# Output projection of a transformer block as seven half-size products, with weight sums made during attention

## The chip, the cores and the metric

One core of a Trainium2 chip runs the whole kernel. The metric is device time in microseconds (us). A core has five engines with instruction queues of their own, each worked through in order: TensorE (PE in the profile; its weight loads are PEld), VectorE (DVE), ScalarE (ACT), GpSimd (POOL) and SyncE (SP), which here issues all DMAs. PSUM, where matmuls accumulate, has eight banks of 128 x 512 fp32 each.

## The reference

An encoder block for 1024 tokens and a model width of 1024, all in fp32. Sixteen meta tokens are put ahead of the sequence and dropped at the end.

```python
def mixer_block(h, w_in, lq1, lk1, lq2, lk2, subln_g, sink, w_ba, w_bb, w_o, lambda_init):
    proj = h @ w_in
    ...
    y_a = differential_attention(...)      # 4 heads: softmax(s1) - lam * softmax(s2), times v
    y_b = windowed_gqa(...)                # 8 heads in a window
    merged = jax.nn.sigmoid(ga) * (y_a @ w_ba) + jax.nn.sigmoid(gb) * (y_b @ w_bb)
    return merged @ w_o

def swiglu(h, w_gate, w_up, w_down):
    return (jax.nn.silu(h @ w_gate) * (h @ w_up)) @ w_down

    # in reference():
        h = h + mixer_block(rms_norm(h, norm_mix[layer]), ...)
        h = h + swiglu(rms_norm(h, norm_ffn[layer]), ...)
    return rms_norm(h, norm_final)[:, N_META:]
```

The change concerns `merged @ w_o`, a product of 1024 x 1024 by 1024 x 1024, and the stages beside it.

## The kernel before

**Numbers.** Every fp32 operand of a large product is kept as a high and a low half in `fp32r`. `split(hi, lo, src, engine)` makes them: ACT copies the high half (L117), the named engine subtracts it from the source to get the low half (L118). Each product is three matmuls: high by high, high by low, low by high.

**Seven products for eight.** The gates (`pg`, L737), the FFN (`product_f`, `pg`, L1293) and the down-projection (`pd`, L1387) are done as 2 x 2 block products with seven half-size multiplications in place of eight (Winograd's form), for which sums of blocks are made of both operands. Before the change the output projection is not: it is a plain product, 8 row tiles x 2 column halves x 8 chunks x 3 = 384 matmuls of 128x512 (`po`, L1070).

**Stages**, in the order of TensorE: projections and branch B's attention (0 to about 322 us); branch A's attention, four heads of eight tiles, interleaved with the gates' matmuls (322 to 622); the branch B product, 16 groups of 12 matmuls (`ppa`, L780); the branch A product, 16 groups, with the merge; the output projection (709 to 801); for each of eight row tiles the second norm and its turn, the transposition into FFN operands (`norm_f`, `turn_f`, `ptn_f`); the FFN in steps of 14 x 11 products with the operands `b` and their sums `t`; the down-projection to the end at 1444.

**A tile of branch A.** TensorE makes scores (`aps`), VectorE takes them with their row maxima, ACT makes the exponentials `as` (L804), POOL scales one of the two maps by lambda (L807), VectorE joins the maps (L810), TensorE transposes the result (`apt`, L822), ACT and VectorE copy it as high and low halves `at` (L825, L826), and TensorE multiplies by the values (`apy`, L835). At the start of a head 30 gate matmuls fill the time in which its first scores pass through the other engines.

**The merge.** For each group `gated` loads a tile of gate logits (`gt`), ACT takes the sigmoid, and VectorE multiplies with the PSUM bank (L1041). POOL adds branch B's part (L1042), and `split` makes the halves of the merged tile `mT`.

**Order.** TensorE's order is the order of the program text from branch A on (`manual_schedule`). ACT, POOL, SP and, before the change, VectorE are ordered by the framework's scheduler, which models the times; the chip then keeps that order. SP's queue is one queue: a DMA that waits holds those behind it. Weight tiles pass through a ring of five raw tiles and eight operand tiles.

The functions that the change touches follow, with the line numbers of the profile.

## Time and profile before

| | |
|---|---|
| Time, median of 3 runs | 1448.48 us (1448.33 to 1451.66) |
| Profiled execution | 1446.1 us, span 1444.3 us |
| Granted TensorE clock | 0.997 |
| Busy: PE, DVE, ACT, POOL | 1422.8, 899.2, 679.6, 641.3 us |
| `po`, output projection | 384 matmuls, 88.0 us |
| `ppa`, branch B and branch A products | 384 matmuls, 622.4 to 709.5 us |

The times are of whole runs; the span is that of the one execution which was profiled. Busy time counts instructions of an engine without its waits. A row of grouped instructions names the line, engine, operation and tiles, then how many, the busy time, the mean of one in ns, and the idle time before them with what ended it. A row of the timeline begins with its start and its length in us.

### The profile page before, as it was taken

Reading aid. Unit: us, or ns where it says so; the run is one execution under the profiler, and the core shown is the slowest. Engines: PE = TensorE matmul, PEld = TensorE weight load, DVE = VectorE, ACT = ScalarE, POOL = GpSimd, SP = SyncE. Lnnn points to the kernel's source line nnn. Section 1 sums busy time; section 2 is a strip of 40 time slices with the busy share of each in tenths; the row PEclk is TensorE's granted clock in tenths of the full one; section 3 lists DMA queues with packets and bytes.
Section 4 is the critical chain, followed back from the end, with each engine's and each line's share of the span. In section 5 each row is a group of like instructions: output and inputs, shape, how many; then the busy total and the mean of one; then the engine's idle time right before and its main releaser. Section 6 shows DMA issues by size and latency. Waiting matters only on the chain.

```text
span 1444.3 us, 21160 instructions
## 1 busy us (share of the span) xinstructions
PE 1422.8 (99%) x7279; PEld 1221.2 (85%) x7279; DVE 899.2 (62%) x1624; ACT 679.6 (47%) x1290; POOL 641.3 (44%) x605
## 2 busy tenths in 40 slices
PE   8999999999999999999999999999999999999997
PEld 6988989988898999888888878888888888888886
DVE  7478536637697989624614966554555553787567
ACT  6366535545665656544413643333333333444454
POOL 5599127743333333334522665544544452000444
PEclk9999999999999999999999999999999999999999
DMA  8467658986557473576612534333332332964443
GB/s 244 90 209 237 193 162 265 288 281 213 190 169 257 147 227 125 190 256 209 216 34 88 152 104 161 109 102 110 102 102 96 110 102 102 331 208 140 124 129 139
DMA packets 188891, 242.41 MB, mean 168 GB/s; under 512 B 18208, under 2 KB 115936, under 8 KB 188784
## 3 DMA queue, kind: packets, MB, share of 16 engines
q1 hardware_dynamic: 188784, 241.07, 52.6%
q8 instruction: 57, 0.93, 0.3%
q14 instruction: 50, 0.41, 0.1%
HBM read 157.45 MB, written 77.00 MB: 162 GB/s over the span
## 4 chain that ended last, share of the span: by engine, by line
PE 81%; POOL 6%; DVE 5%; issue 4%; DMA 2%; ACT 1%; POOLq 0%; SPq 0%; DVEq 0%; ACTq 0%
PE pg L1293 28%; PE pd L1387 9%; PE pg L737 7%; PE po L1070 6%; PE ppa L780 6%; PE aps L796 3%; PE pp_qb L214 3%; POOL oa L118 3%; PE apy L835 3%; PE pp_ka L214 2%; PE pp_va L214 2%; PE apt L822 2%; PE pp_qa L214 2%; PE bpt L356 1%; PE bpy L362 1%
## 5 line engine op out<-in xcount | busy, mean ns | idle before, releaser
L118 POOL TENSOR_TENSOR wop<-wf,wop 128x512 fp32r<-128x512 f32 x128 | 172.6, 1353 | 165.5 <-ACT wop L117 149.6
L1293 PE MATMUL pg<-t,wop 128*128 128x512 f32 x1056 | 242.6, 389 | 0.0
L1293 PEld LDWEIGHTS pg<-t,wop 128*128 128x128 f32 x1056 | 198.3, 188 | 41.1
L1387 PE MATMUL pd<-ob,oa 128*128 128x512 f32 x924 | 209.9, 389 | 0.4 <-POOL oa L118 0.4
L1387 PEld LDWEIGHTS pd<-ob,oa 128*128 128x128 f32 x924 | 173.4, 188 | 36.8 <-POOL oa L118 0.8
L1293 PE MATMUL pg<-b,wop 128*128 128x512 f32 x792 | 185.6, 392 | 2.3 <-DVE c L1302 2.3
L1293 PEld LDWEIGHTS pg<-b,wop 128*128 128x128 f32 x792 | 149.5, 189 | 34.1 <-issue 2.4
L737 PE MATMUL pg<-hT_hi,gop 128*128 128x512 f32 x384 | 142.7, 396 | 0.0
L118 POOL TENSOR_TENSOR oa<-ra,oa 128x512 fp32r<-128x512 f32 x33 | 44.0, 1335 | 170.1 <-ACT oa L117 168.6
L117 ACT ACTIVATE wop<-wf 128x512 fp32r<-128x512 f32 x128 | 80.2, 631 | 82.9 <-PE pg L1293 48.6
L118 POOL TENSOR_TENSOR gop<-gr,gop 128x512 fp32r<-128x512 f32 x48 | 63.3, 1319 | 116.4 <-ACT gop L117 102.6
L117 ACT ACTIVATE oa<-ra 128x512 fp32r<-128x512 f32 x77 | 48.7, 632 | 105.9 <-PE pd L1387 45.1
L804 ACT ACTIVATE as<-as,amn 128x1040 f32<-128x1040 f32 x64 | 74.5, 1164 | 46.9 <-DVE amn L799 42.8
L1128 DVE TENSOR_TENSOR s<-wf,wf 128x512 f32<-128x512 f32 x22 | 25.0, 1138 | 108.1 <-DMA wf<-in_w_ff_gate_dram 58.0
L796 PE MATMUL aps<-ak,aq 128*128 128x392 f32 (+1 forms) x384 | 90.0, 330 | 1.3 <-DVE amn L799 0.6
L1070 PE MATMUL po<-woh,mT 128*128 128x512 f32 x384 | 88.0, 390 | 0.0
L1070 PEld LDWEIGHTS po<-woh,mT 128*128 128x128 f32 x384 | 71.9, 188 | 14.8
L796 PEld LDWEIGHTS aps<-ak,aq 128*128 128x128 f32 x384 | 69.6, 189 | 15.0 <-DVE amn L799 2.2
L737 PEld LDWEIGHTS pg<-hT_hi,gop 128*128 128x128 f32 x384 | 72.7, 189 | 11.2 <-DVE gk L742 0.2
L343 POOL TENSOR_SCALAR bs<-bs,bdn 128x432 f32<-128x432 f32 (+1 forms) x64 | 41.4, 666 | 85.5 <-DVE bdn L341 73.4
L737 PE MATMUL pg<-hT_lo,gop 128*128 128x512 f32 x192 | 76.0, 396 | 0.0
L807 POOL TENSOR_SCALAR as<-as,adn,neglam 128x1040 f32<-128x1040 f32 x32 | 38.8, 1214 | 62.5 <-DVE adn L805 43.9
(287 smaller groups left out, 3099.0 us busy)
## 6 DMA issues: line engine op xcount, KB each, us to landing
ra<-aop SPq DMA_DIRECT2D x77, 256.0 KB, 2.6
wf<-in_w_ff_gate_dram SPq DMA_DIRECT2D x24, 512.0 KB, 4.0
wf<-in_w_ff_up_dram SPq DMA_DIRECT2D x24, 512.0 KB, 3.9
...
w_c<-in_w_in_dram SPq DMA_DIRECT2D x17, 512.0 KB, 5.7
...
ts_d<-to SPq DMA_DIRECT2D x16, 512.0 KB, 3.7
...
```

What stands on the lines that cost most here:

```text
L117: nc.scalar.activation(hi, src, AF.Copy)
L118: lo_eng.tensor_tensor(lo, src, f32(hi), ALU.subtract)
L214: nc.tensor.matmul(ps[:, :n], a[:, c, :], b[:, c, at:at + n], start=(c == 0 and i == 0), stop=(c == DC - 1 and i == 2))
L343: nc.gpsimd.tensor_scalar(st[:, r, :W], st[:, r, :W], dn[:, r:r + 1], 1.0, ALU.mult, ALU.mult)
L737: nc.tensor.matmul(ps, op[:, a, c], quad(b, *act)[:, c], start=(p in (2, 5, 1) and c == 0 and i == 0), stop=(p in (2, 3, 4) and c == 3 and ...
L780: nc.tensor.matmul(ps, w[:, a, j, :], src(j, b, tk), start=(j == 0 and n == 0), stop=(j == 3 and n == 2))
L796: nc.tensor.matmul(ps[:, :n], qs[m][:, t * P:(t + 1) * P], ks[m][:, vv, k0:k0 + n], start=(vv == 0), stop=(vv == 1))
L804: nc.scalar.activation(s[m][:, 0:L], s[m][:, 0:L], AF.Exp, bias=low, scale=-1.0, accum_out=dn[:, m:m + 1])
L835: nc.tensor.matmul(py[:, cols], v[:kp, a, k, :], at_[:kp, k, b, :], start=(k == 0 and j == 0), stop=(k == 8))
L1070: nc.tensor.matmul(ps, mT[:, c, a, t * P:(t + 1) * P], wos[q, c][:, b], start=(c == 0 and n == 0), stop=(c == DC - 1 and n == 2))
L1293: nc.tensor.matmul(ps, op[:, x, c, :], b[:, y, c, :], start=(p in (1, 2, 5) and c == 0 and n == 0), stop=(p in (4, 2, 3) and c == 3 and n ...
L1387: nc.tensor.matmul(ps[u], oa[:, a, u * P:(u + 1) * P], ob[:, b, :], start=(p in (1, 2, 5) and j == 0 and k == 0), stop=(p in (2, 3, 4) and ...
```

## The change

- **Seven products.** `w_o` and the merged tensor are cut in 2 x 2 blocks. Each of seven products (`OUT` = 1, 5, 6, 7, 3, 2, 4) is 4 row tiles x 4 chunks x 3 matmuls = 48, 336 in all, accumulated in three sets of four PSUM banks (`po_x`, `po_y`, `po_z`) and added to the rows `h` at each set's end.
- **Weight sums ahead.** `wo_ahead` is called 16 times during branch A, at every second tile. A call loads a block of `w_o` (the first of four loads two), makes one sum on POOL, splits it (ACT high, POOL low) into `wo_op`, a tile with a single buffer, and stores it to DRAM (`wo_d`). The scheduler places these steps. Products 5, 6, 7 and 3 later load their split weights from there; 1, 2 and 4 load and split blocks of `w_o` as before.
- **VectorE by hand** from the merge to the third feature block of the FFN (step 11). POOL's 16 additions of the merge go to VectorE (`behind`), as do the sums of merged blocks (`m_sum`) and their low halves (`m_low`).
- **Moved.** All low halves of `w_branch_a` and half of those of `ya` are made by POOL; `w_branch_a`'s tiles and the FFN's first weights are loaded from the branch B stage on; the row tiles of `x` are loaded during the merge; the scaling of a normed row is put apart from its norm (`norm_f2`); turns 5, 6 and 7 stand ahead of the FFN's products 0, 1 and 2 (before: 5, 6 and 7 ahead of 0, 2 and 4); the splits of `t` are spread over steps 0 to 10 (`SPLITS`) with their high halves on ACT. PSUM's banks are two groups of four, and an ACT table load is put at the end of the merge.

```diff
+    def wo_ahead(n):
+        c, i = divmod(n, 4)
+        p = (7, 5, 6, 3)[i]
+        tt = nc.gpsimd.tensor_tensor
+        op = vtpool.tile([P, 2, 512], F32R, tag="vt", name=f"wo_op{p}_{c}", bufs=1)
+
+        def block(j, row, col):
+            w = prepool.tile([P, 512], F32, tag=f"w{j}", name=f"wo{j}_{p}_{c}", bufs=1)
+            nc.sync.dma_start(w, w_o[row * P:row * P + P, col * 512:col * 512 + 512])
+            return w
+
+        if i == 0:
+            wo_raw[:] = [block(0, c, 1)]
+        s, b = wo_raw[0], block(1, *{7: (c, 0), 5: (4 + c, 1), 6: (c, 0), 3: (4 + c, 0)}[p])
+        if i == 0:
+            s = f32(op)[:, 1]
+            tt(s, b, wo_raw[0], ALU.subtract)
+        elif i == 1:
+            tt(s, s, b, ALU.add)
+        elif i == 2:
+            tt(s, s, b, ALU.subtract)
+        else:
+            tt(s, b, s, ALU.subtract)
+        split(op[:, 0], op[:, 1], s, nc.gpsimd)
+        nc.sync.dma_start(wo_d[p, c], f32(op))
...
+        if n % 2 and n < AH * NT:
+            wo_ahead(n // 2)
...
-        split(wh[:, 0], wh[:, 1], w, nc.vector if nme == "a" and o >= 4 else nc.gpsimd)
+        wh = p.tile([P, 2, 4, P], F32R, tag="wh", name=f"wbh{nme}_{o}", bufs=WB_BUFS) if nme == "b" else p
+        split(wh[:, 0], wh[:, 1], w, nc.gpsimd)
...
+    OUT = (1, 5, 6, 7, 3, 2, 4)
+    order_o = [(p, c) for p in OUT for c in range(4)]
+    wos, n_wo = {}, [0]
+
+    def prep_wo():
+        if n_wo[0] == len(order_o):
+            return
+        p, c = order_o[n_wo[0]]
+        n_wo[0] += 1
+        op = wos[p, c] = op_tile(f"woh_{p}_{c}")
+        if p in (5, 6, 7, 3):
+            nc.sync.dma_start(f32(op), wo_d[p, c])
+            return
+        row, col = {1: (c, 0), 2: (4 + c, 0), 4: (4 + c, 1)}[p]
+        raw = raw_tile(f"wo_{p}_{c}")[:, 0:512]
+        nc.sync.dma_start(raw, w_o[row * P:row * P + P, col * 512:col * 512 + 512])
+        split(op[:, 0], op[:, 1], raw, nc.gpsimd)
...
+        ws_a[o] = branch_w(wba[o // 4].rearrange("p h c (k n) -> p c h k n", n=P)[:, o % 4], o, w_ba, "a")
+        if o >= 4:
+            prep_wo()
...
+    order_dve = tc.manual_schedule(engines={mybir.EngineType.DVE})
+    order_dve.__enter__()
+    lows = []
+
+    def m_high(p, c, src):
+        hi, lo = m_ops[p][:, 0, c], m_ops[p][:, 1, c]
+        nc.scalar.activation(hi, src, AF.Copy)
+        lows.append(lambda: nc.vector.tensor_tensor(lo, src, f32(hi), ALU.subtract))
+
+    def m_low(n=1):
+        while n > 0 and lows:
+            lows.pop(0)()
+            n -= 1
...
+    def behind():
+        if last:
+            o, half, tk, gt = last.pop()
+            nc.vector.tensor_tensor(tb_row(o, tk), tb_row(o, tk), gt, ALU.add)
+            if o < 4 and half:
+                m_high(1, o, tb_row(o, tk))
+            elif not half:
+                m_sum(5 if o < 4 else 6, o % 4)
...
+    order_a = [(o, half) for b, halves in ((0, (1, 0)), (4, (0, 1))) for half in halves for o in range(b, b + 4)]
     for n, (o, half) in enumerate(order_a):
-        if o not in ws_a:
-            ws_a[o] = branch_w(ypool, o, w_ba, "a")
+        if n == 8:
+            m_ops[6] = half_op(opool, "oc", "mo6")
         gt, ps, tk = gated(1, o, half, ws_a[o], ya)
+        if n < 4:
+            split_ya(0, n, nc.gpsimd)
+        m_low()
+        behind()
         nc.vector.tensor_tensor(gt, gt, ps, ALU.mult)
-        nc.gpsimd.tensor_tensor(gt, gt, tb_row(o, tk), ALU.add)
-        split(mT[:, o, 0, tk], mT[:, o, 1, tk], gt, nc.vector)
-        if n >= 8:
-            prep_wo(0, n - 8)
+        last.append((o, half, tk, gt))
+        if n < 8 and n % 2:
+            prep_wo()
+    table = small.tile([P, 1], F32, tag="ss", name="table")
+    nc.scalar.activation(table, gt[:, 0:1], AF.Silu)
...
+            nc.tensor.matmul(ps, m_ops[p][:, a, c, u * P:(u + 1) * P], wos[p, c][:, b], start=(p in (1, 5, 2) and c == 0 and n == 0),
+                             stop=(p in (3, 2, 4) and c == 3 and n == 2), skip_group_check=True)
...
+        for c in range(4):
+            for u in range(4):
+                out_mm(pss[u], p, u, c)
+            if p == 1 and c == 0:
+                behind()
+            prep_wo()
+            m_low()
+            work.pop(0)()
+        m_low(2)
+        for u in range(4):
+            t, q = {1: (4 + u, 0), 5: (u, 1), 6: (u, 0), 7: (u, 1)}[p]
+            out_add(pss[u], t, q)
...
+    after = {(2, 0): 0, (2, 1): 1, (2, 2): 2, (2, 3): 3, (4, 2): 4, (4, 3): 5}
+    for p in (3, 2, 4):
+        if p == 2:
+            b22 = half_op(apool4, "oa", "b22")
+        for u in range(4):
+            second(p, u)
+            if p == 2 or u:
+                scale_f()
+            if (p, u) in after:
+                turn_f(after[p, u], ("bankA", "bankA"))
+            if p == 3:
+                prep_wo()
...
+    SPLITS = {0: 1, 1: 1, 2: 1, 3: 2, 4: 1, 5: 2, 6: 1, 7: 1, 8: 2, 9: 2, 10: 2}
     for n in range(nf):
-        prepare()
-        if n in AFTER:
-            turn_f(AFTER[n])
-            if n == 0:
-                split_t(0)
-            split_t(AFTER[n] - 4)
-            if AFTER[n] == NT - 1:
-                close_h2()
-                sp, close_spool = pool("spool")
-                spools.append(sp)
-                cp, close_cpool = pool("cpool")
-                cpools.append(cp)
+        if n not in range(4, 8):
+            prepare()
+        if n in (1, 2):
+            turn_f(n + 5)
+        if n == 1:
+            scale_f()
         product_f(*steps[n][1])
         used[0] -= 1
+        low_of(2)
+        for _ in range(SPLITS.get(n, 0)):
+            split_t()
+        if n == 11:
+            low_of(4)
+            order_dve.__exit__(None, None, None)
```

POOL in branch A, the first head's tiles 2 to 5, before. `as_0_2` is L807 of tile 2, `gop` the low half of a gate operand:

```order
L118 TENSOR_TENSOR gop_2_4054<-gr_2_3978,gop_2_4054 128x512
L118 TENSOR_TENSOR gop_3_4127<-gr_3_4052,gop_3_4127 128x512
L807 TENSOR_SCALAR as_0_2_4047<-as_0_2_4047,adn_2_4046,neglam 128x1040
L807 TENSOR_SCALAR as_0_3_4120<-as_0_3_4120,adn_3_4119,neglam 128x1040
L118 TENSOR_TENSOR gop_2_4226<-gr_2_4125,gop_2_4226 128x512
L118 TENSOR_TENSOR gop_3_4298<-gr_3_4224,gop_3_4298 128x512
L807 TENSOR_SCALAR as_0_4_4219<-as_0_4_4219,adn_4_4218,neglam 128x1040
L807 TENSOR_SCALAR as_0_5_4291<-as_0_5_4291,adn_5_4290,neglam 128x1040
```

The same place after (L835 is L807 before, L116 is L118); `wo_7`, `wo_6` and `wo_3` are the blocks and sums of `w_o`, `wo_op` the operand:

```order
L116 TENSOR_TENSOR gop_3_4155<-gr_3_4080,gop_3_4155 128x512
L835 TENSOR_SCALAR as_0_2_4075<-as_0_2_4075,adn_2_4074,neglam 128x1040
L783 TENSOR_TENSOR wo_7_0_4064<-wo_7_0_4064,wo_5_0_4245 128x512
L835 TENSOR_SCALAR as_0_3_4148<-as_0_3_4148,adn_3_4147,neglam 128x1040
L116 TENSOR_TENSOR gop_2_4261<-gr_2_4153,gop_2_4261 128x512
L116 TENSOR_TENSOR wo_op_0_4244<-wo_7_0_4064,wo_op_0_4244 128x512
L785 TENSOR_TENSOR wo_7_0_4064<-wo_7_0_4064,wo_6_0_4423 128x512
L116 TENSOR_TENSOR wo_op_0_4422<-wo_7_0_4064,wo_op_0_4422 128x512
L116 TENSOR_TENSOR gop_3_4333<-gr_3_4259,gop_3_4333 128x512
L787 TENSOR_TENSOR wo_7_0_4064<-wo_3_0_4607,wo_7_0_4064 128x512
L835 TENSOR_SCALAR as_0_4_4254<-as_0_4_4254,adn_4_4253,neglam 128x1040
L116 TENSOR_TENSOR wo_op_0_4606<-wo_7_0_4064,wo_op_0_4606 128x512
```

Between the `as` of tile 3 and that of tile 4 there are now four operations of two calls, beside the gate operands.

SP at the start of the branch B stage, before; `wbrb` are tiles of `w_branch_b`, `raw_ya` and `gt` inputs of the merge:

```order
L997 DMA raw_ya_0_7349<-ya_d_103 128x512
L997 DMA raw_ya_0_7349<-ya_d_104 128x512
L746 DMA g_d_90<-gate_stage 128x512
L997 DMA raw_ya_1_7352<-ya_d_105 128x512
L997 DMA raw_ya_1_7352<-ya_d_106 128x512
L766 DMA wbrb_7355<-in_w_branch_b_dram 128x4x128
L766 DMA wbrb_7397<-in_w_branch_b_dram 128x4x128
L766 DMA wbrb_7439<-in_w_branch_b_dram 128x4x128
```

And after, with tiles of `w_branch_a` (`wbra`) and the FFN's first operands (`gp`) between them:

```order
L794 DMA wbra_7465<-in_w_branch_a_dram 128x4x128
L1036 DMA raw_ya_0_7503<-ya_d_103 128x512
L744 DMA g_d_90<-gate_stage 128x512
L1036 DMA raw_ya_0_7503<-ya_d_104 128x512
L1036 DMA raw_ya_1_7506<-ya_d_105 128x512
L1036 DMA raw_ya_1_7506<-ya_d_106 128x512
L794 DMA wbra_7509<-in_w_branch_a_dram 128x4x128
L794 DMA wbrb_7513<-in_w_branch_b_dram 128x4x128
L1091 DMA gp<-in_norm_ffn_dram 128x1024
L1048 DMA gt_2_0_7518<-g_d_77 128x512
L1208 DMA gp<-in_w_ff_gate_dram 128x8x128
L1208 DMA gp<-in_w_ff_up_dram 128x8x128
```

The third tile of `w_branch_b` (the first `wbrb` here) has moved behind two tiles of `w_branch_a`.

VectorE at the turns, before; `xn_f` is the scaling of a normed row, `h` the addition of a product to the row, `b` the low half of a turn:

```order
L1204 SCALAR_TENSOR_TENSOR xn_f_8514<-h_2_8048,rstd_f_8517,gffn 128x1024
L1204 SCALAR_TENSOR_TENSOR xn_f_8523<-h_3_8050,rstd_f_8526,gffn 128x1024
L1075 TENSOR_TENSOR h_4_8052<-h_4_8052,po_4_8531 128x512
L1223 TENSOR_TENSOR b_8041<-ptn_f_0_8566,b_8041 128x4x128
L1223 TENSOR_TENSOR b_8042<-ptn_f_1_8574,b_8042 128x4x128
L1204 SCALAR_TENSOR_TENSOR xn_f_8557<-h_4_8052,rstd_f_8560,gffn 128x1024
L1075 TENSOR_TENSOR h_5_8054<-h_5_8054,po_5_8582 128x512
L1223 TENSOR_TENSOR b_8041<-ptn_f_0_8617,b_8041 128x4x128
L1223 TENSOR_TENSOR b_8042<-ptn_f_1_8625,b_8042 128x4x128
L1204 SCALAR_TENSOR_TENSOR xn_f_8608<-h_5_8054,rstd_f_8611,gffn 128x1024
```

And after:

```order
L1174 TENSOR_TENSOR h_3_8174<-h_3_8174,po_y_8343 128x512
L1307 SCALAR_TENSOR_TENSOR xn_f_8634<-h_2_8172,rstd_f_8637,gp 128x1024
L1174 TENSOR_TENSOR h_4_8160<-h_4_8160,po_z_8674 128x512
L1307 SCALAR_TENSOR_TENSOR xn_f_8660<-h_3_8174,rstd_f_8663,gp 128x1024
L1325 TENSOR_TENSOR b_8482<-ptn_f_0_8690,b_8482 128x4x128
L1325 TENSOR_TENSOR b_8567<-ptn_f_1_8698,b_8567 128x4x128
L1174 TENSOR_TENSOR h_5_8162<-h_5_8162,po_z_8706 128x512
L1325 TENSOR_TENSOR b_8482<-ptn_f_0_8721,b_8482 128x4x128
L1325 TENSOR_TENSOR b_8567<-ptn_f_1_8729,b_8567 128x4x128
L1174 TENSOR_TENSOR h_6_8164<-h_6_8164,po_z_8737 128x512
```

The scaling of row 3 now stands between the addition of row 4's first half and the low halves of row 0's turn.

222 lines of the change are left out of this document (139 added, 83 removed).

## Prediction

> **What bounds the kernel now.** I read the page's head first, then the table of busy time by stage, then TensorE's own waits, then single rows where the change puts work.
>
> ```profile
> span 1444.3 us, 21160 instructions
> PE 1422.8 (99%) x7279; PEld 1221.2 (85%) x7279; DVE 899.2 (62%) x1624; ACT 679.6 (47%) x1290; POOL 641.3 (44%) x605
> L1070 PE MATMUL po<-woh,mT 128*128 128x512 f32 x384 | 88.0, 390 | 0.0
> ```
>
> TensorE works 99% of the span, and the 384 products of the output projection (`po`) had no idle time before them. A matmul taken from TensorE is therefore time saved, and any wait that the change gives TensorE is time lost. The stages, with each engine's busy time:
>
> ```profile
> 322.00:622.00 300.00, 295.56 (x1772) 264.61 (x1771) 232.47 (x656) 174.29 (x326) 113.25 (x93) 0.99 0.58 192
> 622.00:665.50 43.50, 43.50 (x193) 35.98 (x192) 12.72 (x19) 19.71 (x33) 14.08 (x11) 1.00 0.73 232
> 665.50:709.20 43.70, 43.70 (x195) 36.18 (x194) 28.86 (x34) 23.30 (x40) 28.97 (x20) 1.00 0.65 197
> 709.20:801.00 91.80, 91.80 (x428) 76.52 (x427) 33.19 (x42) 27.11 (x49) 25.93 (x28) 1.00 0.27 98
> 801.00:834.00 33.00, 30.71 (x146) 25.12 (x144) 31.03 (x37) 20.11 (x36) 23.62 (x16) 0.99 0.60 168
> 834.00:1000.00 166.00, 166.00 (x727) 137.33 (x727) 100.68 (x113) 63.62 (x111) 90.24 (x66) 0.99 0.36 115
> ```
>
> The columns are stage, length, then busy time of PE, PEld, DVE, ACT and POOL, granted clock, DMA share, GB/s. Rows one to five are branch A with the gates, the branch B product, the branch A product with the merge, the output projection, and the last norms with the first FFN products. TensorE is full in four of the six. Only branch A (4.4 us free) and 801 to 834 (2.3 us free) have gaps, and in the latter VectorE is busy 31.03 of 33 us. Who ends TensorE's waits, from 622 to 835 (first row) and in branch A (second):
>
> ```profile
> PE pg L1293 <- DVE c L1302: 2.3, 2, 2.0
> PE apt L822 <- DVE as L810: 2.6, 2, 1.9
> ```
>
> So everything from the merge to the FFN can gain at most the matmuls removed plus 2.3 us.
>
> **Output projection (gain).** Before, 384 matmuls of 88.0 / 384 = 0.229 us. Seven products of 48 make 336. The 48 that go are worth 48 x 0.229 = 11.0 us, and nothing hides them: **-11.0**. This term has one answer.
>
> **Merge.** POOL's 16 additions go to VectorE, which now does four operations per group of 12 matmuls (multiply, low half, add, sum). What one costs depends on POOL:
>
> ```profile
> 801.21 1.77 DVE L1236 TENSOR_TENSOR kept<-kept,ts 128x512 f32<-128x512 f32 x1
> 807.73 0.68 DVE L1235 TENSOR_TENSOR kept<-ts,kept 128x512 f32<-128x512 f32 x1
> 808.33 0.69 DVE L1236 TENSOR_TENSOR kept<-kept,ts 128x512 f32<-128x512 f32 x1
> L118 DVE TENSOR_TENSOR mT<-gt,mT 128x512 fp32r<-128x512 f32 x16 | 17.8, 1113 | 14.7 <-ACT mT L117 14.5
> L1042 POOL TENSOR_TENSOR gt<-gt,tb 128x512 f32<-128x512 f32 x8 | 12.4, 1564 | 3.0 <-DVE gt L1041 3.0
> ```
>
> Alone, one starts every 0.60 us; beside POOL a two-tensor operation takes 1.1 to 1.8. Four alone are 2.4 us and 12 matmuls 43.7 / 16 = 2.73, so VectorE keeps pace where POOL is idle. POOL has some eight operations left in the first half of the merge (four low halves of `ya`, four of weights), so VectorE falls back by about (0.6 + 3 x 1.11) - 2.73 = 1.2 us a group over four groups, 5 us. Four banks of a tag cover three groups, 8 us. I take **0**; if each of the eight held VectorE for its whole 1.3 us, 10.4 against 8 would leave 2.4 (0 to 2.4). ACT's extra table load at the merge's end lies in a stage where ACT works 23.30 of 43.70 us: 0.
>
> **Operands and loads.** Four of the seven products load their 16 split weight tiles (512 KB each) from DRAM, one product ahead in a ring of eight. Four tiles are 2 MB, 6.9 us at the 306 GB/s that the next fence's last row shows, against 11.0 us of a product, in a stage whose DMA share is 0.27; the row tiles of `x` come earlier, through the same queue: **0**. Without that cover a product would wait the missing part of 6.9 us.
>
> **Branch B stage.** SP now issues two tiles of `w_branch_a` (512 KB together) ahead of the third tile of `w_branch_b`:
>
> ```profile
> 622.43 87.08 PE ppa L780 x384
> 630.16 0.63 ACT L117 ACTIVATE wbhb<-wbrb 128x512 fp32r<-128x512 f32 x1 [0.27 <-DMA wbrb<-in_w_branch_b_dram]
> 630.87 5.07 POOL L118 TENSOR_TENSOR wbhb<-wbrb,wbhb 128x512 fp32r<-128x512 f32 x4 [14.12 <-ACT wbhb L117]
> 300.00:322.00 22.00, 22.00 (x107) 18.56 (x106) 5.94 (x9) 9.49 (x16) 10.51 (x17) 1.00 0.96 306
> ```
>
> The third tile is ready at 630.87 + 5.07 / 4 = 632.1 and needed after 48 matmuls, at 622.43 + 48 x 0.227 = 633.3. That is 1.2 us to spare; 512 KB at a full 306 GB/s cost 1.7. **+0.5** (0 to 2).
>
> **Turns and the first FFN products.** Here VectorE's order is now written out. The wait on `c` stood behind these low halves of `t`:
>
> ```profile
> L118 DVE TENSOR_TENSOR t<-ts,t 128x512 fp32r<-128x512 f32 x8 | 7.6, 975 | 0.8 <-ACT t L117 0.8
> L118 DVE TENSOR_TENSOR t<-kept,t 128x512 fp32r<-128x512 f32 x4 | 4.3, 1077 | 0.0
> 833.56 393.55 PE pg L1293 x1728
> ```
>
> The twelve, 11.9 us in all, are now spread over the FFN's first eleven products: **-2.3** (0 to -2.3). In its place three short waits are possible. Each row norm is a chain:
>
> ```profile
> 793.84 0.69 DVE L1075 TENSOR_TENSOR h<-h,po 128x512 f32<-128x512 f32 x1 [1.38 <-PE po L1070]
> L1202 ACT ACTIVATE xn_f<-h 128x1024 f32<-128x1024 f32 x8 | 8.4, 1053 | 25.5 <-DVE h L1075 19.9 <-issue 5.6
> L122 POOL TENSOR_SCALAR rstd_f<-ss_f 128x1 f32<-128x1 f32 x8 | 4.7, 585 | 33.6 <-ACT xn_f L1202 33.4
> 797.04 1.28 DVE L1204 SCALAR_TENSOR_TENSOR xn_f<-h,rstd_f,gffn 128x1024 f32<-128x1024 f32 x1
> ```
>
> From the end of the products at 793.8 to the scaled row at 798.3 it takes 4.5 us. In product 2 the scaling of row 3 stands on VectorE ahead of the low halves of row 0's turn, and behind ACT's copies of the last weights; a bank for the next turn comes free only after them: about 2 us of wait (0 to 3). Turns 6 and 7 come one FFN product (12 x 0.229 = 2.75 us) after their rows with five or six VectorE operations ahead: 0.4 + 0.6 (0 to 3). The product at step 12 needs weight sums that VectorE reaches only late; by the same walk 1.3 us are left, so 0 (0 to 4). Together **+3.0** (0 to 10). Behind that the FFN's 393.55 us without a wait, in the row above, and the down-projection keep their order: 0.
>
> **Branch A (the new work).** Sixteen calls add 32 POOL operations, 16 ACT copies, 20 loads of 256 KB and 16 stores of 512 KB, packed by the scheduler into about 18 of 32 tiles. On sums there is room: POOL 113.25 + 32 x 1.32 = 155 of 300 us, ACT 174 + 10, and 13.6 MB over some 175 us is 78 GB/s beside 192. What costs is order. All calls share one operand tile, so ACT's copy and POOL's subtraction of a call wait for the store of the call before, and what stands behind them waits too. At tile 4 of the first head two calls stand ahead of its `as`:
>
> ```profile
> L118 POOL TENSOR_TENSOR gop<-gr,gop 128x512 fp32r<-128x512 f32 x48 | 63.3, 1319 | 116.4 <-ACT gop L117 102.6 <-DVE amn L799 10.0 <-PE pg L737 3.7
> ts_d<-to SPq DMA_DIRECT2D x16, 512.0 KB, 3.7
> 352.89 1.22 POOL L807 TENSOR_SCALAR as<-as,adn,neglam 128x1040 f32<-128x1040 f32 x1 [4.07 <-PE apt L822]
> 354.06 1.29 POOL L118 TENSOR_TENSOR gop<-gr,gop 128x512 fp32r<-128x512 f32 x1
> 362.22 1.23 POOL L807 TENSOR_SCALAR as<-as,adn,neglam 128x1040 f32<-128x1040 f32 x1 [0.23 <-DVE adn L805]
> 364.88 1.30 DVE L810 SCALAR_TENSOR_TENSOR as<-as,adn,as 128x1040 f32<-128x1040 f32 x1
> 366.59 0.60 PE L822 MATMUL apt<-ident,as 128*128 128x128 f32 x4
> L810 DVE SCALAR_TENSOR_TENSOR as<-as,adn,as x32: 1279/1301/2244, 336.7 to 589.6; 128x1040 f32<-128x1040 f32 x32
>   DVE as L810: 6.2, 7
> 430.59 1.29 DVE L810 SCALAR_TENSOR_TENSOR as<-as,adn,as 128x1040 f32<-128x1040 f32 x1
> 434.50 0.60 PE L822 MATMUL apt<-ident,as 128*128 128x128 f32 x4
> ```
>
> POOL is free of tile 3 at 354.1; gate operand 1.3 and low half 1.3 bring 356.7; the store lands 3.7 later, 360.4; ACT's copy 0.6, 361.0; then low half, gate operand and next sum, 3 x 1.3, 364.9; `as` ends at 366.1, where it ended at 363.4. VectorE's L810 then ends at 367.4 and the transposes, at 366.59 before, come 0.8 us late. Tile 6, with a like queue, I put at 1.7, and the ten calls of the later heads at 1.0, since a tile there has more to spare (434.50 - 431.88 = 2.6 us in the last two rows): **+3.5**. The ends are 0 (stores as quick as the fastest, all in gaps) and 10 (0.6 for each of the 16).
>
> **Sum.** -11.0 - 2.3 + 0.5 + 3.0 + 3.5 = -6.3. The profiled run took 1446.1 us (1.8 beside its span), so it becomes 1439.8; the median of the three runs is 2.4 above that run, so the forecast is **1442.2**. About 0.3% (4.3 us) is what a measurement of this kernel can tell from no change: 1444.1 and 1452.8 are the bounds.
>
> **Rivals.**
> - *Everything is hidden*: stores land in gaps, and the order by hand waits nowhere. -11.0 - 2.3 + 0.2 gives 1435.4. For it: POOL is idle 62% of branch A. Against: the walk at tile 4.
> - *VectorE's order waits at its upper prices*: 3 + 3 + 4 in the turns, 2 in the branch B stage, and 3.5 in branch A. -13.3 + 12 + 3.5 = +2.2, 1450.7: no change. For it: VectorE was busy 94% there. Against: its longest row of work there, the twelve low halves, is gone.
> - *VectorE and POOL hold each other in branch A.* L810 reads two tensors and has taken up to 2.24 us, 0.94 over its median; the transposes already wait for it in 7 tiles of 32. Held there each time by an added POOL operation it costs 7 x 0.94 = 6.6 on top of the forecast: 1448.8, no change. The Trainium skill ("SBUF — State Buffer", section on the two separate sides) has it that a VectorE operation with two SBUF inputs and a GpSimd one lock each other out for a whole instruction. By that rule the merge, too, would lose its upper price; the rows of 1.77 against 0.69 us agree with it.
> - *Branch A becomes slower than the projection gains.* The round of store, copy, subtraction (3.7 + 0.6 + 2.6 = 6.9 us) is nearly the pitch of a tile (300 / 32 = 9.4), the next head's loads (about 3 MB, some 10 us at 306 GB/s) stand ahead of a store in SP's queue at each head, and exponentials queue behind ACT's waiting copy. At 1.3 us a round, 16 rounds cost 20.8 instead of 3.5: +11.0, 1459.5, slower. It decides from 3.5 + 6.3 + 4.3 = 14.1 us, 0.9 a round. Against: at each head 30 gate matmuls, 30 x 0.227 = 6.8 us, are kept to fill the gap.
>
> **Chances.** Forecast 0.47, of which 0.40 below 1444.1 and 0.07 within the bounds; all hidden 0.17; the order by hand 0.09; the hold 0.07; branch A slower 0.20. So faster 0.57, same 0.23, slower 0.20. The forecast's own range is 1437 to 1447. The range reaches down to all hidden, 1435, and up through the two cases of no change into the slower one, 1455.
>
> **What would show it.** Right: 336 `po` matmuls of about 77 us; no wait of TensorE over 1 us between 665 and 700; no 2 us wait on `c`; branch A's stage 3 to 4 us longer, ended by `as` or by ACT behind a copy into `wo_op`. Wrong: TensorE's idle time from branch A's start to step 12 above 19 us, or a steady FFN that is not 393 us long.

## The result, and the profile after

The changed kernel takes 1455.71 us (median of 8 runs, 1451.64 to 1459.29) against 1448.40 us before (8 runs, 1447.20 to 1451.66): a ratio of 1.0044, 95% interval 1.0033 to 1.0055. It is slower by 6 to 7 us; 1442.2, which is 6 us faster, was forecast. The profiled execution took 1459.29 us, the slowest of the eight, so its stages show somewhat more than the median does: its span is 13.2 us longer, 1.9 of them in the first 323 us, which the change does not touch.

The head of the changed kernel's page, and its stages, cut at the same places as the table below (branch A from the first gate matmul, branch B product, branch A product, projection with its turns to the first FFN product, FFN). Columns as in the prediction: stage, length, busy time of PE, PEld, DVE, ACT, POOL, granted clock, DMA share, GB/s:

```profile
span 1457.5 us, 21230 instructions
PE 1423.1 (98%) x7231; PEld 1211.8 (83%) x7231; DVE 937.6 (64%) x1672; ACT 694.5 (48%) x1315; POOL 666.6 (46%) x625
```

```profile
324.73:634.58 309.85, 297.81 (x1769) 264.14 (x1768) 238.15 (x656) 183.27 (x342) 159.83 (x125) 0.99 0.70 229
634.58:681.41 46.83, 44.20 (x193) 35.80 (x192) 13.18 (x19) 23.60 (x38) 22.77 (x18) 1.00 0.95 303
681.41:726.04 44.63, 44.63 (x194) 36.18 (x193) 34.07 (x51) 19.25 (x32) 6.27 (x5) 1.00 0.61 218
726.04:811.81 85.77, 83.64 (x385) 69.15 (x384) 50.33 (x70) 35.14 (x63) 21.26 (x26) 0.98 0.38 129
811.81:1238.91 427.10, 425.34 (x1868) 348.31 (x1866) 257.61 (x280) 165.31 (x288) 214.98 (x156) 1.00 0.35 113
```

And of the kernel before:

```profile
322.88:622.26 299.38, 294.94 (x1769) 264.10 (x1768) 232.47 (x656) 174.55 (x327) 113.25 (x93) 0.99 0.58 191
622.26:665.82 43.56, 43.56 (x194) 36.04 (x193) 12.72 (x19) 19.45 (x32) 14.08 (x11) 1.00 0.73 232
665.82:709.34 43.52, 43.52 (x193) 36.03 (x192) 29.00 (x34) 23.30 (x40) 28.97 (x20) 1.00 0.65 197
709.34:801.64 92.30, 92.30 (x433) 77.06 (x432) 33.69 (x43) 27.11 (x49) 26.57 (x28) 1.00 0.26 97
801.64:1226.94 425.30, 423.01 (x1867) 349.76 (x1866) 247.89 (x277) 167.46 (x289) 216.07 (x158) 1.00 0.36 113
```

| Stage, us | before | after | after_pad224 | after_one_call_pad | both orders mended |
|---|---|---|---|---|---|
| branch A | 299.4 | 309.9 | 308.0 | 301.5 | 306.5 |
| branch B product | 43.6 | 46.8 | 47.1 | 45.7 | 43.6 |
| branch A product, merge | 43.5 | 44.6 | 43.5 | 43.5 | 43.7 |
| projection, turns | 92.3 | 85.8 | 84.1 | 85.7 | 83.2 |
| FFN | 425.3 | 427.1 | 423.4 | 423.5 | 423.5 |

(The last three columns are kernels of the experiments. 1.7 us of a stage can be chance: in these profiles TensorE also ran for 3.4 us at half clock behind a wait of about 2 us, in the FFN of before and in the projection of after and of after_one_call_pad, but in neither stage of the other two.) TensorE has 48 matmuls less, yet it is busy 1423.1 us where it was 1422.8: those that are left take longer. Branch A and the branch B product lost 13.7 us, and the projection gained 6.5. The six longest of TensorE's waits from 320 to 870, by what ended them:

```profile
PE apt L850 <- DVE at L854: 2.9, 2, 2.7
PE ppa L808 <- POOL wbhb L116: 2.6, 2, 1.5
PE apt L850 <- DVE as L838: 2.6, 2, 1.9
PE ptn_f L1320 <- ACT kept L1327: 2.1, 1, 2.1
PE aps L824 <- DMA ak<-ka_d: 1.5, 2, 1.3
PE pg L735 <- ACT at L853: 1.4, 1, 1.4
```

The 2.6 us on `as` were there before. Of the wait on `c`, 0.3 us is left; the one on `kept` is product 2's turn, `wbhb` is the branch B stage, and the rest of these six is branch A.

### The profile page after: what moved, and what is told of

Same layout as the page of the kernel before. It is cut to its first block, busy times and chain, and to the rows that moved or that the text cites. A ratio compares the mean times of both kernels' runs of the same rounds, so it can differ in the third digit from the quotient of the medians.

```text
span 1457.5 us, 21230 instructions
## 1 busy us (share of the span) xinstructions
PE 1423.1 (98%) x7231; PEld 1211.8 (83%) x7231; DVE 937.6 (64%) x1672; ACT 694.5 (48%) x1315; POOL 666.6 (46%) x625
## 5 line engine op out<-in xcount | busy, mean ns | idle before, releaser
L116 POOL TENSOR_TENSOR wop<-wf,wop 128x512 fp32r<-128x512 f32 x128 | 174.3, 1367 | 171.6 <-ACT wop L115 158.0
L1445 PE MATMUL pg<-t,wop 128*128 128x512 f32 x1056 | 246.5, 392 | 0.4 <-DVE copies_p L1459 0.4
L116 POOL TENSOR_TENSOR oa<-ra,oa 128x512 fp32r<-128x512 f32 x33 | 44.1, 1337 | 170.8 <-ACT oa L115 169.3
L116 POOL TENSOR_TENSOR gop<-gr,gop 128x512 fp32r<-128x512 f32 x48 | 63.7, 1329 | 79.4 <-ACT gop L115 77.3
L824 PEld LDWEIGHTS aps<-ak,aq 128*128 128x128 f32 x384 | 68.9, 188 | 18.6 <-DVE amn L827 4.2
L331 DVE CUSTOM_DVE_ANT_0 bs<-bps,tbx,nsink 128x432 f32<-128x432 f32 (+1 forms) x64 | 38.2, 622 | 37.4 <-PE bps L329 28.4
L863 PE MATMUL apy<-at,av 128*128 128x256 f32 x400 | 59.5, 292 | 0.3 <-DVE at L854 0.3
L827 DVE CUSTOM_DVE_ANT_0 as<-aps,dist,far_a 128x392 f32<-128x392 f32 x64 | 39.6, 619 | 31.1 <-PE aps L824 30.8
```

The lines of the kernel that those rows point to most:

```text
L116: lo_eng.tensor_tensor(lo, src, f32(hi), ALU.subtract)
L331: nc.vector.tensor_tensor_reduce(st[:, r, :W], ps[:, :W], tb, 2.0 ** -(4 * g + r + 1), nsink[:, 4 * g + r:4 * g + r + 1], ALU.add, ALU.min ...
L824: nc.tensor.matmul(ps[:, :n], qs[m][:, t * P:(t + 1) * P], ks[m][:, vv, k0:k0 + n], start=(vv == 0), stop=(vv == 1))
L827: nc.vector.tensor_tensor_reduce(s[m][:, k0:k0 + n], ps[:, :n], far_by, slope, low, ALU.add, ALU.min, mn[:, m, i:i + 1])
L863: nc.tensor.matmul(py[:, cols], v[:kp, a, k, :], at_[:kp, k, b, :], start=(k == 0 and j == 0), stop=(k == 8))
L1445: nc.tensor.matmul(ps, op[:, x, c, :], b[:, y, c, :], start=(p in (1, 2, 5) and c == 0 and n == 0), stop=(p in (4, 2, 3) and c == 3 and n ...
```

## What the experiments showed

All are compared with the kernel before, run beside them on the same chip (medians 1448.64 to 1448.93).

### Two causes, undone one at a time

`PAD` is the length of an unused tile ahead of the pools on the right side of SBUF. Padding moves their addresses by 128 bytes and leaves every instruction in its place. In both kernels the edit is

```diff
-PAD = 96
+PAD = 224
```

On the changed kernel:

> The changed kernel with PAD 96 -> 224, so that every tile of the right-hand pools lies 128 bytes lower; the order of the instructions is the same. Theory A (weights and moving operand whose SBUF addresses differ modulo 256 bytes are multiplied at 0.233 us a matmul in place of 0.227): the branch A product, product 2 and the FFN products 6 and 5 return to 0.227, 192 x 0.0057 + 48 x 0.0058 + 528 x 0.0067 = 4.9 us faster than the changed kernel, about 1450.8. Rival B (the slower pace comes from traffic on SBUF at that time, or from the run): no change, 1455.7, and the same groups still at 0.233.

Measured 1449.17 us (11 runs), ratio 0.9999 (0.9990 to 1.0008): 6.5 us come back. On the kernel before:

> The kernel before with PAD 96 -> 224. Here the FFN's three operands b lie in a left-hand pool and their weights in the right-hand ring, all 128 modulo 256 now; moved by 128 bytes, weights and b differ. Theory A: the 792 matmuls of pg<-b go from 0.227 to 0.233, +5.0 us, about 1453.4, and nothing else changes pace. Rival B: no change, 1448.4.

Measured 1453.08 us, ratio 1.0030 (1.0019 to 1.0042): the kernel before becomes slower by the same edit. Groups of matmuls of the changed kernel (columns: line, engine, operation, tiles, shapes, count, busy time, mean ns, idle time):

```profile
L1445 PE MATMUL pg<-t,wop 128*128 128x512 f32 x1056 | 246.5, 392 | 0.4 <-DVE copies_p L1459 0.4
L1445 PE MATMUL pg<-b,wop 128*128 128x512 f32 x792 | 183.7, 390 | 0.3 <-DVE c L1454 0.3
L808 PE MATMUL ppa<-ya,wba_od 128*128 128x512 f32 x96 | 22.5, 395 | 0.0
```

The same with 128 bytes more:

```profile
L1445 PE MATMUL pg<-t,wop 128*128 128x512 f32 x1056 | 242.9, 389 | 0.6 <-DVE copies_p L1459 0.6
L1445 PE MATMUL pg<-b,wop 128*128 128x512 f32 x792 | 183.7, 390 | 0.0
L808 PE MATMUL ppa<-ya,wba_od 128*128 128x512 f32 x96 | 21.9, 389 | 0.0
```

And the kernel before, as it was and with 128 bytes more:

```profile
L1293 PE MATMUL pg<-b,wop 128*128 128x512 f32 x792 | 185.6, 392 | 2.3 <-DVE c L1302 2.3
L1293 PE MATMUL pg<-b,wop 128*128 128x512 f32 x792 | 188.6, 395 | 1.7 <-DVE c L1302 1.7
```

The groups that changed are those in which one operand lies on the right side and the other on the left. By the built programs' addresses (bytes in a partition, modulo 256), the ring and the right side lie at 128; of the changed kernel's operands, `ya` of both halves, product 2's merged half, and `t_6` and `t_5` of the FFN lie on the left at 0, while their partners lie at 128. With `PAD` = 224 all of these agree. Before, every such pair agreed, until the padding moved the ring away from `b11`, `b21` and `b22`. From the starts of successive matmuls in the traces, a pair that agrees goes on every 0.2267 us, one that differs by 128 every 0.232 to 0.2335, 2.5 to 3.0% more. Half of the 1056 `pg<-t` are such: at 0.0066 on average, 528 of them make 3.5 us, and the two rows differ by 3.6. With the merge (1.1) and product 2 (0.3) that is 5.0 of the 6.5 us; the other 1.5 cannot be placed, and the intervals of the two ratios leave about 2 us open.

Agreement is not the whole rule, though. In the kernel before, the matmuls of `hT` (gates and first projections) have weights at 64 and `hT` at 0, 64, 128 or 192. They start every 0.2315 to 0.233 us, and the quarter whose addresses agree, at 64, is no quicker than that: 0.2316. No run varies what sets their pace.

The other cause, the calls of `wo_ahead`: one instead of 16, so that all 16 ready operands are the same sum and 15 of the sums are left out.

```diff
-        if n % 2 and n < AH * NT:
-            wo_ahead(n // 2)
+        if n == 1:
+            wo_ahead(0)
...
-            nc.sync.dma_start(f32(op), wo_d[p, c])
+            nc.sync.dma_start(f32(op), wo_d[7, 0])
```

> The changed kernel with one call of wo_ahead in place of 16, and all 16 ready operands loaded from that one store: it leaves the weight sums of the other 15 out (so the output is not the reference's); what follows branch A is unchanged. Theory C (the calls' order and transfers are what lengthens branch A, 310 us against 300): branch A back at 300 to 301, about 9 us faster than the changed kernel, 1446.5. Rival D (branch A is longer because of jitter or of a lower clock in that run): less than 3 us.

Measured 1448.29 us, 0.9996 (0.9987 to 1.0004): 7.4 us. With both edits:

> Both edits in one: one call of wo_ahead (15 weight sums left out) and PAD 224. Theories A and C together: 4.9 + 9 us under the changed kernel, about 1441.8, so the sum of the two effects; then the rest, 1448.4 - 1441.8 = 6.6, is what the seven products gain after their own waits (-11.0 - 2.3 + 2.6 + 3.9 = -6.8). If A or C is wrong, higher by its amount.

Measured 1441.92 us, 0.9954 (0.9942 to 0.9966). The two effects add. That their sum ends at the forecast of 1442.2 is luck: this kernel has one call, while the forecast counted 3.5 us for sixteen, and the loss in the branch B stage is still in it.

### What of a call costs

All of these stand on after_pad224 (1449.17 us, branch A 305.3 us from its first scores; with one call 298.7; the table counts 2.8 us of gate matmuls ahead of the scores to branch A). Three profiled executions with unchanged branch A code (after_pad224 and the first two of the next section) gave 303.6 to 307.2, so a single stage length is good to about 2 us. The granted clock has a part in this: the shortest of the three has no stretch at half clock in branch A, after_pad224 one of 3.4 us, and the longest 10.2 us in all.

Spread over all tiles, by taking the calls' second block from the ring of the gates' raw tiles:

```diff
-            w = prepool.tile([P, 512], F32, tag=f"w{j}", name=f"wo{j}_{p}_{c}", bufs=1)
+            w = gpool.tile([P, 512], F32, tag="gr", name=f"wo{j}_{p}_{c}", bufs=GR_BUFS) if j else prepool.tile([P, 512], F32, tag="w0", name=f"wo{j}_{p}_{c}", bufs=1)
```

> On top of after_pad224: block(1) of each weight sum is loaded into the ring of branch A's raw tiles instead of a buffer of its own, so that the 16 calls are spread over the 32 tiles of branch A (four to a head) instead of lying in the first 17. The same work is done. Theory I (density: the calls cost because four passes of 512 by 128 a call crowd VectorE, ScalarE and GpSimd while a tile has 9.6 us): with half the density, branch A loses less than half of its 7 us, and the time falls by 3 to 5 us, to 1444.2 to 1446.2. Rival J (each call costs its 0.45 us wherever it lies): branch A stays at 305 us from its first transpose and the time at 1449.2; a ring slot fewer for the raw tiles could make it worse.

Measured 1456.84 us, 1.0051 (1.0035 to 1.0067), branch A 312.4: worse than either theory. Spreading the calls in this way does not help; since they now also take slots from the gates' ring, the run does not price density by itself.

Short stores:

```diff
-        nc.sync.dma_start(wo_d[p, c], f32(op))
+        n_col = 512 if n == 0 else 16
+        nc.sync.dma_start(wo_d[p, c][:, :, 0:n_col], f32(op)[:, :, 0:n_col])
...
-            nc.sync.dma_start(f32(op), wo_d[p, c])
+            nc.sync.dma_start(f32(op), wo_d[7, 0])
```

> On top of after_pad224: the stores of the sums are cut from 512 columns to 16 from the second call on, and every ready operand of the seven products is loaded from the one place that is still stored in full; this leaves most of the stored sums out of the computation. The VectorE, ScalarE and GpSimd passes of the calls stay. Theory K (the store holds the one operand buffer, so that the next call's passes bunch up and fall on the wrong side of a tile's own): branch A loses 3 us or more less, and the time is 1446 or below. Rival L (the passes themselves are the cost): no change beyond 1 us, 1449.2.

Measured 1453.74 us, 1.0032 (1.0019 to 1.0045), branch A 306.9. It is 4.6 us slower than after_pad224, which neither K nor L foresaw: storing fewer bytes gains nothing. But the edit did not take away the wait that K is about. ScalarE's copies into `wo_op` still stood 10.1 us (3 times) for a store to land, against 11.3 us (5 times) in after_pad224, because a short store took up to 9.8 us to land (a full one up to 9.1). So the run does not decide whether the round of store, copy and subtraction, on which the prediction's walk and its slower rival were built, is part of what a call costs.

ScalarE taken out of the calls (`split` done by two GpSimd passes):

```diff
-        split(op[:, 0], op[:, 1], s, nc.gpsimd)
+        nc.gpsimd.tensor_copy(op[:, 0], s)
+        nc.gpsimd.tensor_tensor(op[:, 1], s, f32(op[:, 0]), ALU.subtract)
```

> On top of after_pad224: the 16 copies that round a weight sum into its high half go from ScalarE to GpSimd, so that ScalarE has no part in the calls; GpSimd gets 16 passes more. Theory M (ScalarE: its copies into wo_op wait, by the trace, for a store or for GpSimd's sum, 16.6 us in all, and exponentials and copies into at queue behind them): branch A falls from 305.3 us by 3 us or more, and the time to 1446 or below. Rival N (GpSimd: what costs are its passes, which stand ahead of its scaling of as and lie beside VectorE's L838): branch A grows by 2 us or more, and the time to 1451 or above.

Measured 1451.21 us, 1.0014 (1.0003 to 1.0026), branch A 306.6: slightly worse, and M falls; rival N's time is met, its 2 us in branch A are not quite (1.3). GpSimd's passes taken out:

```diff
...
-            tt(s, b, s, ALU.subtract)
-        split(op[:, 0], op[:, 1], s, nc.gpsimd)
-        nc.sync.dma_start(wo_d[p, c], f32(op))
+        s = b
+        nc.scalar.activation(op[:, 0], s, AF.Copy)
+        for k in range(2):
+            nc.sync.dma_start(wo_d[p, c][:, k], f32(op)[:, 0])
```

> On top of after_pad224: the calls lose GpSimd's passes (the 16 sums and the 16 low halves are left out of the computation); one block is loaded in each call, ScalarE copies it into wo_op's high half, and that half is stored twice, so that ScalarE's copies, the one operand tile and the bytes stored stay. Theory N (GpSimd's passes): branch A falls to within 2 us of the 298.7 us of after_one_call_pad, and the time to 1442 to 1444. Rival M (ScalarE's copies, stores): branch A stays above 302, and the time above 1446.

Measured 1455.54 us, 1.0052 (1.0032 to 1.0071), branch A 310.4. N falls as it was put. Ahead of the stores SP's queue now waits 27.5 us (to 500) for ScalarE's copies, where in the changed kernel it waited 12.2 us for GpSimd's low halves; what makes the whole slower stays open. So the opposite was tried, the passes without DMAs:

```diff
-        if i == 0:
-            wo_raw[:] = [block(0, c, 1)]
-        s, b = wo_raw[0], block(1, *{7: (c, 0), 5: (4 + c, 1), 6: (c, 0), 3: (4 + c, 0)}[p])
+        if n == 0:
+            wo_raw[:] = [block(0, c, 1), block(1, c, 0)]
+        s, b = wo_raw
...
-        nc.sync.dma_start(wo_d[p, c], f32(op))
+        if n == 0:
+            nc.sync.dma_start(wo_d[p, c], f32(op))
...
-            nc.sync.dma_start(f32(op), wo_d[p, c])
+            nc.sync.dma_start(f32(op), wo_d[7, 0])
```

> On top of after_pad224: the 16 calls keep their GpSimd and ScalarE passes at the same places, but from the second call on they have no load and no store (all work on the first call's two blocks; the products load one stored operand; so 15 of the 16 sums are left out). Theory Q (the calls cost by their DMAs: 20 loads and 16 stores in SP's one queue, ahead of the gates' loads and the next head's, which took the DMA share from 62% to 84% between 325 and 480): branch A falls from 305.3 to within 2 us of 298.7, the time to 1442 to 1444. Rival R (the passes are the cost after all, on either engine): branch A stays above 303, the time above 1447.

Measured 1445.56 us, 0.9980 (0.9971 to 0.9989), branch A 302.2: midway, 3.6 us under after_pad224 and 3.6 over after_one_call_pad. **With the loads and stores of all calls but the first taken away, about half of the calls' price goes, and half stays with the passes.** These are not two prices that stand by themselves. The passes also moved: the last low half of a call starts at 426.6 us, in after_pad224 at 486.7. And after_pad_no_pool_passes has the loads and stores without the passes and is 13.6 us over after_one_call_pad, more than all calls cost with both. The DMAs from 325 to 480, the hardware queue's packets, MB and share of 16 engines, in the kernel before and in the changed one:

```profile
q1 hardware_dynamic: 17413, 31.90, 62.0%
```

```profile
q1 hardware_dynamic: 21233, 42.19, 83.5%
```

Without the calls' DMAs it is 62.9%. One way in which the passes cost is seen in one place of the changed kernel, tile 6 of the first head (timeline: start, length, engine, line, operation, idle time before):

```profile
379.39 1.29 POOL L783 TENSOR_TENSOR wo<-wo,wo 128x512 f32<-128x512 f32 x1 [0.88 <-DMA wo<-in_w_out_dram]
380.64 1.29 POOL L116 TENSOR_TENSOR gop<-gr,gop 128x512 fp32r<-128x512 f32 x1
381.90 1.03 POOL L879 TENSOR_TENSOR af<-af,neg_half 128x4 f32<-128x4 f32 x1
382.94 1.22 POOL L835 TENSOR_SCALAR as<-as,adn,neglam 128x1040 f32<-128x1040 f32 x1
384.13 1.26 POOL L116 TENSOR_TENSOR wo_op<-wo,wo_op 128x512 fp32r<-128x512 f32 x1
385.47 2.15 POOL L785 TENSOR_TENSOR wo<-wo,wo 128x512 f32<-128x512 f32 x1
384.19 2.30 DVE L838 SCALAR_TENSOR_TENSOR as<-as,adn,as 128x1040 f32<-128x1040 f32 x1 [1.49 <-POOL as L835]
387.24 0.63 PE L850 MATMUL apt<-ident,as 128*128 128x128 f32 x4 [2.72 <-DVE at L854]
```

A sum, a gate operand and a small operation stand ahead of GpSimd's scaling of `as`, and VectorE's L838 waits 1.49 us for that; then a call's low half starts 0.06 us ahead of L838, which takes 2.30 us instead of 1.30, and the next sum, begun while it runs, 2.15 instead of 1.29. The low half of `at` behind it is late, and TensorE stands 2.72 us. That is the third rival's mechanism. Neither before nor after_one_call_pad has a wait of over 1.2 us in this place. But L838 in all took 45.3 us in 32 (44.3 before), far from the 6.6 us more that the rival asked for; and after_pad_short_stores, which has no such wait here either, is slower all the same. So this is one meeting that costs, and not an account of the whole half.

The calls' DMAs on GpSimd's queue:

```diff
-            nc.sync.dma_start(w, w_o[row * P:row * P + P, col * 512:col * 512 + 512])
+            nc.gpsimd.dma_start(w, w_o[row * P:row * P + P, col * 512:col * 512 + 512])
...
-        nc.sync.dma_start(wo_d[p, c], f32(op))
+        nc.gpsimd.dma_start(wo_d[p, c], f32(op))
```

> On top of after_pad224: the calls' 20 loads and 16 stores are issued by GpSimd instead of SP, so that SP no longer stands waiting for a call's pass (12.2 us in front of the stores, 9.3 us in front of the loads, in the changed kernel up to 500) with the gates' and the next head's loads behind it. The bytes stay. Theory Q1 (SP's order): branch A falls by 4 us or more, the time to 1445 or below. Theory Q2 (the bytes): no change beyond 2 us, 1447 to 1451. Rival S: issuing costs GpSimd time of its own, and branch A grows: 1452 or above.

Measured 1458.53 us, 1.0063 (1.0050 to 1.0076), branch A 313.0: rival S. TensorE's waits on VectorE's `as`, which depends on GpSimd, show it:

```profile
PE apt L850 <- DVE as L838: 11.2, 4, 8.6
```

The Trainium skill ("DMA: Bandwidth & Descriptors", section "Issuing engines are not separate DMA queues") says that a second issuing engine saves only the time to issue; here it lost 9.4 us. Whether the DMA half is the bytes, their place in SP's queue or the waits of the passes for them stays open.

### The two smaller terms

Behind `w_branch_b`'s tiles instead of ahead:

```diff
-        ws_a[o] = branch_w(wba[o // 4].rearrange("p h c (k n) -> p c h k n", n=P)[:, o % 4], o, w_ba, "a")
+        for k in {4: (0,), 5: (1, 2), 6: (3, 4), 7: (5, 6, 7)}.get(o, ()):
+            ws_a[k] = branch_w(wba[k // 4].rearrange("p h c (k n) -> p c h k n", n=P)[:, k % 4], k, w_ba, "a")
```

> On top of after_pad224: the loads of w_branch_a, which in the changed kernel stand ahead of w_branch_b's tiles 4 to 7 in SP's row, are issued behind them (one, two, two and three tiles behind tiles 4, 5, 6 and 7). Theory E (SP's order): TensorE's two waits of 1.51 and 1.12 us on wbhb in the changed kernel's branch B stage come from those loads; the stage falls from 47.1 us in after_pad224 to about 44.5, and the time by 2.6 us, to 1446.6. Rival F (the wait comes from w_branch_b's own three transposing transfers, whatever stands ahead of them): the waits stay, and the time is within 1 us of 1449.2.

Measured 1448.46 us, 0.9992 (0.9980 to 1.0004). The stage falls to 43.6 us, without a wait, so E holds; 0.8 and 0.5 us of it come back in the next two stages, and a net 2.3 us is too little to be seen in the whole time.

Row 0's turn ahead of row 3's scaling:

```diff
-            if p == 2 or u:
+            if p != 2 and u:
                 scale_f()
             if (p, u) in after:
                 turn_f(after[p, u], ("bankA", "bankA"))
+            if p == 2:
+                scale_f()
```

> On top of after_pad224: in product 2 row 0's turn stands ahead of row 3's scaling on VectorE, as it does in no other place of the changed kernel. Theory G (the order that the prediction read from the rows): TensorE's wait of 2.1 us on kept goes, and the time falls by 2.1 us, to 1447.1; if the granted clock's dip that followed that wait goes too, by up to 1.7 us more, to 1445.4. Rival H: row 3's turn, later now by its scaling, takes over the wait, 1 to 2 us at a later product, and the time stays within 1 us of 1449.2.

Measured 1447.78 us, 0.9993 (0.9982 to 1.0004). Of the 2.2 us wait on `kept`, two of 0.3 us are left, and no other took its place; projection and turns fall by 1.5 us. Both together:

> after_pad224 with both changes of order: the loads of w_branch_a behind w_branch_b's, and row 0's turn ahead of row 3's scaling. In their own runs the stages from branch B to the first FFN product fell by 2.2 and 1.5 us against after_pad224. If both add: 1449.2 - 3.7 = 1445.5. Rival (the waits only move): 1447.5 or above.

Measured 1445.73 us (11 runs), 0.9977 (0.9968 to 0.9986). They add, and **this version is faster than both kernels**: all seven products and all sums, with the padding and the two changes of order. Its stages, from branch A on:

```profile
323.12:629.65 306.53, 296.69 (x1770) 264.07 (x1768) 238.76 (x656) 183.78 (x343) 159.40 (x125) 0.99 0.70 232
629.65:673.20 43.55, 43.55 (x194) 36.04 (x192) 12.60 (x19) 22.17 (x36) 20.57 (x16) 1.00 0.97 313
673.20:716.86 43.66, 43.66 (x194) 35.97 (x192) 32.83 (x49) 19.62 (x33) 8.49 (x6) 1.00 0.66 234
716.86:800.07 83.21, 82.23 (x386) 67.88 (x384) 51.76 (x73) 35.26 (x63) 21.33 (x26) 1.00 0.39 134
800.07:1223.59 423.52, 421.74 (x1867) 348.39 (x1866) 255.13 (x280) 165.68 (x288) 216.49 (x156) 1.00 0.35 114
```

### The sums at another place

The kernels of this section also have `PAD` = 224 and both changes of order. The sums made while the projection runs, with no call in branch A (in `prep_wo`; the other three products' sums alike):

```diff
-            nc.sync.dma_start(f32(op), wo_d[p, c])
+            raw = raw_tile(f"wo_{p}_{c}")
+            s, b = raw[:, 0:512], raw[:, 512:]
...
+            elif p == 5:
+                block(s, c, 1)
+                block(b, 4 + c, 1)
+                tt(s, s, b, ALU.add)
...
+            split(op[:, 0], op[:, 1], s, nc.gpsimd)
```

> The same seven products and the same sums, without the 16 calls in branch A: each weight sum is made by GpSimd while the output projection runs, two products ahead, from raw blocks, with the running sum kept in DRAM (256 KB each) between products 5, 6 and 3; with the loads of w_branch_a behind w_branch_b, row 0's turn ahead of row 3's scaling, and the padding of 224 bytes. From after_one_call_pad's 1441.9: minus 2 to 3.5 in the branch B stage, minus 1.5 in the turns: 1437 to 1439, if branch A is as long as there (298.7 us) and GpSimd's 1.3 us a pass (two a tile) keep ahead of a product's 2.7 us a tile. Rival: GpSimd is idle from 700 to 758 in after_pad224, but its passes now lie beside VectorE's in the merge and the products; TensorE then waits on woh in products 5 to 3, up to 1 us a tile, 16 us: 1445 to 1455.

Measured 1448.55 us, 0.9996 (0.9986 to 1.0007). Branch A is 299.8 us from its first scores, as hoped, 4.0 us less than in the version above, but the merge and the projection take 135.6 us, 8.7 more than there. In the merge GpSimd's sums and VectorE's operations lie side by side again:

```profile
689.43 1.74 POOL L1052 TENSOR_TENSOR wo<-wo 128x512 f32<-128x512 f32 x1
688.25 1.77 DVE L1126 TENSOR_TENSOR tb<-tb,gt 128x512 f32<-128x512 f32 x1
696.75 0.68 DVE L1126 TENSOR_TENSOR tb<-tb,gt 128x512 f32<-128x512 f32 x1
```

and TensorE's waits have

```profile
PE po_x L1164 <- DVE gt L1141: 5.4, 3, 3.8
```

L1126 takes 1.77 us beside GpSimd and 0.68 alone; VectorE ends the merge late, and the first products wait 5.4 us for its banks. It is the mechanism to which the prediction gave at most 2.4 us in the merge.

Product 5's sums alone moved back into branch A (four calls), so that the merge has fewer:

> As after_local_sums, but product 5's four sums are made in branch A (four calls, each with two loads, one sum, one split and two stores) so that GpSimd has no sum in the merge, where its passes held VectorE: the 5.4 us of waits at the start of the projection and 0.8 in the merge go, and branch A gives back four calls at 0.45, 1.8: 1448.6 - 6.2 + 1.8 = 1444.2. Rival: product 6's sums, now first in the ring, are still made in the merge, and VectorE is late as before: 1448 to 1451.

Measured 1447.16 us (12 runs, 1444.27 to 1452.25), 0.9996 (0.9983 to 1.0008). The wait at the projection's start falls to 2.8 us, not to 0, because product 6's sums moved up into the merge; the whole time cannot be told from before. With the sums of products 6, 7 and 3 held back by their buffer (`s` from the tag `gt`, the gates' tiles, in place of a raw tile):

> after_hybrid_sums, with the sums of products 6, 7 and 3 made in the buffers of the merge's gates, so that GpSimd can begin them only when VectorE's merge is almost done. Theory (GpSimd's sums beside VectorE's operations in the merge): the 2.8 us of waits at the projection's start go, and the 0.6 us a product behind them; branch B, the merge and the projection become 43.5 + 43.5 + 57.2 us; time 1447.2 - 3.3 = 1443.9. Rival: the sums of product 6, later now, are late for TensorE: 1447 or above.

Measured 1448.97 us, 1.0003 (0.9994 to 1.0013). The theory's stages hold (43.55, 43.52 and 57.67 us up to the first turn), but the rows of `h` are then late for the first turns (1.3 us on `h`, 2.2 us on `kept`, with 3.4 us at half clock behind it), which take 29.9 us where after_hybrid_sums took 25.4.

## Why the prediction was wrong, by its own steps

- **Output projection, -11.0: right.** 48 matmuls less; projection and turns fell by 6.5 us, which with the 2.1 us of wait and the 1.7 of half clock in this stage is 10.3. In after_pad224, without that stretch of half clock, it is 8.2 + 2.2 = 10.4.
- **Wait on `c`, -2.3: right.** 0.3 us of it is left, and with the padding none; the FFN is then 423.4 us, 1.9 under before, where the stretch at half clock is part of the difference and turns 6 and 7 wait inside this stage.
- **Turns, +3.0: right.** Product 2's wait was 2.1 us (about 2), turns 6 and 7 waited 0.46 and 0.64 (0.4 and 0.6), from the order read on VectorE. The turn moved ahead took away nearly all of the first.
- **Merge, 0: right as to waits.** VectorE kept pace. Its stage was still 1.1 us longer, by the pace of its matmuls.
- **Branch B stage, +0.5: mis-sized.** 3.3 us. The step took two tiles of `w_branch_a` at a full rate of 306 GB/s against 1.2 us to spare, and looked at the third tile of `w_branch_b` alone. TensorE waited 1.51 us for that one and 1.12 for the fourth: on SP's queue one more tile of `w_branch_a` stands ahead of each later tile of `w_branch_b`, and the stage runs at a DMA share of 0.95. With the loads in the other order the stage is back at 43.6 us. The upper end of the range given for it, 2, was too low as well.
- **Branch A, +3.5: mis-sized, 7.3.** The step that failed is "on sums there is room": it costed the order alone, the passes and the wait for one store, and set the 13.6 MB at nothing, since 78 GB/s beside 192 seemed to fit. Without the loads and stores, the passes alone left 3.6 us; the other 3.6 go with the loads and stores. That the first figure is near the 3.5 of the walk is in part luck: the walk has a store's landing in it, which those passes do not wait for.
- **"The FFN ... and the down-projection keep their order: 0": the step that was missing.** The order was kept, the addresses were not. The sum took 0.229 us for every matmul, whatever its operands, and 6.5 us of the miss come from there. In before all operand pairs of the products behind branch A agreed, so their rows did not show it; but the page of before has a slower group of the same shape, the gates (the FFN's `pg<-t` has a mean of 389 ns there):

```profile
L737 PE MATMUL pg<-hT_hi,gop 128*128 128x512 f32 x384 | 142.7, 396 | 0.0
```

It could have been asked why, since the change moves operands to other pools. The prediction did name the sign, an FFN that is not 393 us long: it was 396.1. Its other sign, TensorE idle above 19 us, did not come: 18.6 us from branch A's start to 870.

The distance is 1455.7 - 1442.2 = 13.5 us: 6.5 of pace, 3.8 in branch A, 2.8 in the branch B stage, and 0.4 left. Of the rivals none came true as written. The slower one, to which 0.20 was given, named one of the stages, with 7.3 instead of the 14.1 that it needed; whether its round of stores has a part in the 7.3 no run settles.
